# Attention of a mixer put in another order, and matmul results held in PSUM tiles of two banks

## The chip, the cores and the metric

One core of one Trainium2 chip runs the whole program. The metric is the device time of one execution in microseconds (us), the median of several runs. A separate execution of the same program was profiled; all rows below come from that one.

## The reference

A trunk of two layers over 256 tokens of width 1024, all float32. Each layer is: half a SwiGLU block (width 2816), a hybrid mixer, half a SwiGLU block; a last RMSNorm ends it. Cut to the mixer:

```python
def hybrid_mixer(h, w_in, b_forget, g_kv, w_kv_up, g_idx_k, w_up_fox, w_up_sb, w_up_dsa, w_out, cos, sin):
    (q_a, k_a, v_a, f_a, q_b, k_b, v_b, q_c, c_kv, q_i, k_i, w_i, gates) = jnp.split(h @ w_in, _split_points(), axis=-1)
    y_a = forgetting_attention(heads(q_a, N_HEADS_FOX), heads(k_a, N_HEADS_FOX), heads(v_a, N_HEADS_FOX), f_a + b_forget)
    y_b = stick_breaking_attention(heads(q_b, N_HEADS_SB), heads(k_b, N_HEADS_SB), heads(v_b, N_HEADS_SB))
    k_c, v_c = jnp.split(rmsnorm(c_kv, g_kv) @ w_kv_up, 2, axis=-1)
    ...
    y_c = dsa_attention(q_c, k_c, v_c, q_i, k_i, w_i)
    g_a, g_b, g_c = jnp.split(jax.nn.sigmoid(gates), N_BRANCH, axis=-1)
    merged = g_a * (y_a @ w_up_fox) + g_b * (y_b @ w_up_sb) + g_c * (y_c @ w_up_dsa)
    return merged @ w_out
```

Forgetting attention ("fox" in the kernel) adds to its scores the difference of cumulated log-sigmoids of the forget logits `f_a`. Stick-breaking attention ("stick") weighs by a cumulated sum of log-sigmoids along the keys. The sparse attention ("dsa") keeps, for each query, the keys with the largest indexer scores.

## The kernel before

**Weights.** Every weight matrix is read from HBM once, in chunks of columns. SyncE's queue brings float32 pieces into four `raw` buffers; ScalarE writes their f16 high part `whi` (L251), VectorE the remainder `wlo` (L253), into seven buffers each. A piece is 128x2048 at most. TensorE multiplies activations, split the same way, by both parts: three matmuls of 256 columns for each 128x128 block of weights (`project_T`, L339), or the same with tokens as rows (`project`, L374 to L376).

**Products and PSUM.** A product of 512 weight columns fills two PSUM tiles of one bank each (`banks_of` takes two of the four buffers of `mmt`). Each tile is evicted by an instruction of its own, up to 512 columns wide: the gate (L658) and the product with the up half (L665) of the feed-forward block (FFN), the scaling of projections (L809, L811), the gating of the mixer's three up-projections (L1172). Attention scores take the two `at` buffers, the small results the two `tp` buffers.

**Order in a mixer.** The input projection `w_in` runs in eight groups (`IN_GROUPS`): indexer, dsa queries and latent, fox keys, fox queries, fox values with forget logits, stick queries, stick keys, stick values; then six chunks of gates (`gt`), the three up-projections `up` in two halves each, and the output projection `o`. Attention is written as tasks (generators); after every two k-tiles of a weight product `background()` lets each task take one step up to its next `yield`. So a task's instructions land between those of the products, and the number of `yield`s sets how far behind its inputs a step stands on each engine. The forget task (from L947) turns the forget logits into `kb` (L974) and `qb` (L977), which the first matmuls of each fox score `sa` need; the indexer task ends in eight iterations of top-k, MAX8 (L913) and MATCH_REPLACE8 (L914) on two spans each. The stick heads wait in a chain: score `sb`, three exponential and logarithm steps on ScalarE (`eb`), `lb` and `hb` (L1087, L476), cumulated sum `cb` (L1096), exp, values `yb` (L989), split into `y`. The sigmoids of the gates (L1160) come after the last of them, since they need another table of ScalarE.

**Start and end.** The first chunk's x and weights come in small pieces; of the second chunk (`ci == 1`) four pieces of 128x1024 are read. The row scale `Rf` of the first norm (L551) is copied on ScalarE during the second chunk, and the first gates (L658) need it. Gains of later norms are loaded at about 56 us (`grow`, L465) and transposed on TensorE (`gps`, L417). At the very end the last chunk of the down-projection is made with tokens as rows, first the rows of token tile 0, then those of tile 1, in two PSUM tiles `d0768` and `d1768`; each has a residual step (L695), a norm and a store.

Of the kernel before, what the change touches and what calls it, by code (L numbers as in the profile page):

```python
# [20 lines left out]
P = 128  # L21
D = 1024
SEQ = 256
# [26 lines left out]
IN_GROUPS = [(QI, 324), (QC, 448), (KA, 384), (QA, 384), (VA, 390), (QB, 384), (QB + 384, 256), (VB, 320)]  # L50
# [79 lines left out]
def trunk(ctx, tc, io, out, flag):  # L130
# [22 lines left out]
    def mmt(name):  # L153
        return pp.tile([P, 512], F32, tag="mm", bufs=4, name=name)
# [45 lines left out]
    RAW_BUFS, HL_BUFS = (4, 6) if wide else (4, 7)  # L200
# [151 lines left out]
    def banks_of(n, nm):  # L352
        return [mmt(f"{nm}_{i}") for i in range((n // P + 1) // 2)]
# [48 lines left out]
    grow0 = cp.tile([16, P], F32, tag="grow0", name="grow0")  # L402
    grow1 = cp.tile([34, P], F32, tag="grow1", name="grow1")
# [19 lines left out]
    def warm_up(n, *first):  # L423
        ps = mmt("warm")
        for i in range(n):
            behind(nc.tensor.matmul(ps[:, :P], ident, ident, start=True, stop=True), *first)
# [15 lines left out]
    def const(nm, shape, dt=F32):  # L442
# [4 lines left out]
    mask_a, mask_b, tri, negu, fsel, rope_c, rope_s = (  # L447
        late.append(const(nm, shape, dt)) or late[-1][0] for nm, shape, dt in (
            ("mask_a", [P, P], BF16), ("mask_b", [P, 2 * P], BF16), ("tri", [P, 2, SEQ], F32), ("negu", [P, P], F32),
# [6 lines left out]
             (wkv, io["w_kv_up"].rearrange("l k n -> k l n")),  # L456
             (grow1[:16, :], io["g_mix"].rearrange("l (k p) -> (l k) p", p=P)),
             (grow1[16:32, :], io["g_ffn2"].rearrange("l (k p) -> (l k) p", p=P)),
             (grow1[32:34, :], io["g_kv_latent"])]
# [22 lines left out]
    class Norm:  # L482
# [16 lines left out]
        def half(self, h):  # L499
# [3 lines left out]
            with tc.high_priority():  # L503
                for k in range(4 * h, 4 * h + 4):
                    self.parts(k, xT[:, k, :])
# [31 lines left out]
        def scales(self, ms):  # L537
# [8 lines left out]
            yield  # L546
            yield
# [88 lines left out]
    def ffn(l, gu, dn, norm, nxt):  # L636
# [4 lines left out]
        def parts(s, c, n):  # L641
            for (i, j, w), st in zip(widths(n), s):
                j += c // P
                split(ah[:, j:j + w, :], al[:, j:j + w, :], pair(st, w), 1.0 / (sw * sx), note())
                yield

        for c, n in FF_CHUNKS:
            nm = f"{gu}{l}_{c}"
            g = banks_of(n, "g" + nm)
# [12 lines left out]
            u = banks_of(n, "u" + nm)  # L662
            project_T(gu, l, DFF + c, n, (norm.hi, norm.lo), u, gate)
            for i, _, w in widths(n):
                nc.vector.tensor_tensor(s[i][:, :w * SEQ], u[i][:, :w * SEQ], s[i][:, :w * SEQ], op=ALU.mult)  # L665
            done[c // P] = Task(parts(s, c, n))
# [11 lines left out]
        if nxt is not None:  # L678
            for c, n in down_chunks(dn, l):
                d = banks_of(n, f"d{c}{dn}{l}")  # L680
                project_T(dn, l, c, n, (ah, al), d, ready)
                with tc.high_priority():
                    for i, b, w in widths(n):
                        add_T(c // P + b, w, d[i], norm.by_row(w))
                nxt.half(c // 512)
# [4 lines left out]
        for c, n in down_chunks(dn, l):  # L690
            d = [mmt(f"d{t}{c}{dn}{l}") for t in range(NT)]
# [84 lines left out]
    def mixer(l, norm, nxt):  # L776
# [12 lines left out]
        def group(c, n, parts):  # L789

            ps = [mmt(f"in{c}_{t}_{l}") for t in range(NT)]
# [10 lines left out]
        def group_T(c, n):  # L802
            ps = banks_of(n, f"in{c}_{l}")
            project_T("w_in", l, c, n, (norm.hi, norm.lo), ps)
            return ps
# [72 lines left out]
        def indexer():  # L878
# [7 lines left out]
            yield  # L886
            yield
# [3 lines left out]
            for j in range(2):  # L891
                ps = blocks(f"iqp{j}{l}", [(t, PQI + j * P, P) for t in range(NT)])
                Ts = [halves(ps, r, f"iq{j}{r}{l}") for r in (0, HD)]
                yield
# [14 lines left out]
            nc.vector.memset(sc[:CHUNK, P + 3 * CHUNK:3 * P], NEG)  # L909
            for i in range(TOPK // 8):  # L910
# [4 lines left out]
                yield  # L915
# [135 lines left out]
        def dsa_heads(heads, nm):  # L1051
# [7 lines left out]
            for _ in range(3):  # L1059
                yield  # L1060
# [8 lines left out]
        def stick_heads(heads, nm):  # L1069
# [5 lines left out]
            for _ in range(3):  # L1075
# [44 lines left out]
        for g, at, eighth in ((2, 3, False), (3, 0, True)):  # L1120
            ps = group_T(*IN_GROUPS[g])
            for i, j, w in widths(WA):
                scaled(qk[:, at + j:at + j + w, :], pair(ps[i], w), norm.by_row(w), eighth)
# [8 lines left out]
        ps = group_T(*IN_GROUPS[5])  # L1132
# [5 lines left out]
        ps = group_T(*IN_GROUPS[6])  # L1138
        scaled(qk[:, 9:11, :], pair(ps[0], 2), norm.by_row(2), False)
# [5 lines left out]
        for i in range(6):  # L1145
            ps = banks_of(512, f"gt{i}_{l}")
            project_T("w_in", l, GATES + i * 512, 512, (norm.hi, norm.lo), ps)
            for j, b, w in widths(512):
                scaled(gt[:, 4 * i + b:4 * i + b + w, :], pair(ps[j], w), norm.by_row(w), False)
# [29 lines left out]
        for h in range(2):  # L1179
            ps = banks_of(512, f"o{h}_{l}")  # L1180
            project_T("w_out", l, h * 512, 512, (mh, ml), ps)
            with tc.high_priority():
                for i in range(2):
                    xs = xT[:, 4 * h + 2 * i:4 * h + 2 * i + 2, :]
                    nc.vector.scalar_tensor_tensor(xs, pair(ps[i], 2), 1.0 / (sw * sm), xs, op0=ALU.mult, op1=ALU.add)
            nxt.half(h)
# [67 lines left out]
```

## Time and profile before

| | us |
|---|---|
| median of 3 runs (1174.01 to 1174.45) | 1174.4 |
| the profiled execution's own time | 1174.17 |
| its span in the trace | 1172.4 |
| TensorE busy | 1126.7 |
| VectorE busy | 776.4 |
| ScalarE busy | 617.2 |
[...]

Some 1.8 us of the profiled execution lie outside the span. TensorE is busy for 96% of it, but this is an average: in the FFNs it never stops, and the time in which it stands lies in the first 35 us, in the two mixers and in the last 20 us. Busy counts a matmul that runs at half the clock as well, so a stretch can be busy and slow.

### The profile page before, as it was taken

What the parts mean: (1) busy time and instruction counts of PE and PEld (TensorE: products, weight loads), DVE (VectorE), ACT (ScalarE), POOL (GpSimd) and SP (SyncE); (2) the same over time, 40 slices, a digit from 0 to 9 for tenths busy, and PEclk for the clock granted to TensorE, in tenths of its full rate; (3) what the DMA queues carried; (4) which work ended last, traced back from release to release, by engine and by line L of the source; (5) the groups of instructions that cost most, each with busy time, mean ns of one, the idle gap of its engine ahead of it and who ended that gap; (6) DMA issues with size and microseconds to landing.
All of it is one profiled execution on the core that took longest, in us unless ns stands there. A gap on an engine that the chain in (4) does not pass through costs nothing. (4 is left out here: it accounts for less than half of the span.)

```text
span 1172.4 us, 22850 instructions
## 1 busy us (share of the span) xinstructions
PE 1126.7 (96%) x9744; PEld 962.4 (82%) x9744; DVE 776.4 (66%) x1341; ACT 617.2 (53%) x833; POOL 12.9 (1%) x25
## 2 busy tenths in 40 slices
PE   9999999989998999999999999999899989999996
PEld 7888886767886888888888888867688778988765
DVE  5966556996656966575575565579856779655632
ACT  7745435756657564454444363366566575544520
POOL 0000000000000000000000000010000000000000
PEclk9999999999998999999999999999899989999999
DMA  8956656554342765576665575555533437555701
GB/s 294 371 185 200 219 167 193 168 183 159 110 144 73 246 202 169 176 236 199 213 205 167 168 250 164 162 189 184 179 118 118 144 107 253 180 163 195 245 29 40
DMA packets 118772, 209.96 MB, mean 179 GB/s; under 512 B 4819, under 2 KB 43909, under 8 KB 118661
## 3 DMA queue, kind: packets, MB, share of 16 engines
q1 hardware_dynamic: 118340, 207.88, 54.9%
q8 instruction: 78, 1.28, 0.4%
q10 hardware_dynamic: 320, 0.53, 0.1%
q14 instruction: 34, 0.27, 0.1%
HBM read 207.35 MB, written 1.05 MB: 178 GB/s over the span
## 5 line engine op out<-in xcount | busy, mean ns | idle before, releaser
L253 DVE SCALAR_TENSOR_TENSOR wlo<-raw,whi 128x2048 f16<-128x2048 f32 (+5 forms) x218 | 446.6, 2050 | 254.7 <-ACT whi L251 254.5
L339 PEld LDWEIGHTS <-whi 128*128 128x128 f16 x5504 | 539.0, 98 | 69.5 <-issue 5.9
L251 ACT ACTIVATE whi<-raw 128x2048 f16<-128x2048 f32 (+5 forms) x218 | 374.0, 1718 | 409.1 <-issue 95.7
L339 PEld LDWEIGHTS <-wlo 128*128 128x128 f16 x2768 | 271.6, 98 | 38.7 <-issue 4.8
L339 PE MATMUL gw_ffn_gu<-xThif,whi 128*128 128x256 f16 x704 | 191.6, 273 | 1.2 <-DVE s0w_ffn_gu L658 1.2
L339 PE MATMUL gw_ffn_gu<-xTlof,whi 128*128 128x256 f16 x704 | 191.7, 273 | 0.8 <-DVE xTlof L496 0.8
L339 PE MATMUL gw_ffn_gu<-xThif,wlo 128*128 128x256 f16 x704 | 191.5, 273 | 1.0 <-DVE wlo L253 0.9
L339 PE MATMUL uw_ffn_gu<-xThif,whi 128*128 128x256 f16 x704 | 191.9, 273 | 0.0
L339 PE MATMUL uw_ffn_gu<-xThif,wlo 128*128 128x256 f16 x704 | 191.9, 273 | 0.0
L339 PE MATMUL uw_ffn_gu<-xTlof,whi 128*128 128x256 f16 x704 | 191.9, 273 | 0.0
L339 PE MATMUL gt<-xTlomx,whi 128*128 128x256 f16 x384 | 104.7, 273 | 0.0
L339 PE MATMUL gt<-xThimx,wlo 128*128 128x256 f16 x384 | 104.7, 273 | 0.0
L339 PE MATMUL gt<-xThimx,whi 128*128 128x256 f16 x384 | 104.7, 273 | 0.0
L339 PE MATMUL d0w_ffn_down<-ahw_ffn_gu,whi 128*128 128x256 f16 x264 | 72.0, 273 | 0.0
L339 PE MATMUL d512w_ffn_down<-alw_ffn_gu,whi 128*128 128x256 f16 x264 | 72.0, 273 | 0.0
L339 PE MATMUL d0w_ffn_down<-ahw_ffn_gu,wlo 128*128 128x256 f16 x264 | 72.0, 273 | 0.0
L339 PE MATMUL d512w_ffn_down<-ahw_ffn_gu,whi 128*128 128x256 f16 x264 | 72.0, 273 | 0.0
L339 PE MATMUL d0w_ffn_down<-alw_ffn_gu,whi 128*128 128x256 f16 x264 | 72.0, 273 | 0.0
L339 PE MATMUL d512w_ffn_down<-ahw_ffn_gu,wlo 128*128 128x256 f16 x264 | 72.0, 273 | 0.0
L339 PE MATMUL up<-y,whi 128*128 128x256 f16 x256 | 48.6, 285 | 4.1 <-DVE gt L1172 2.5
L339 PE MATMUL in<-xThimx,whi 128*128 128x256 f16 x176 | 48.0, 273 | 0.0
L339 PE MATMUL in<-xThimx,wlo 128*128 128x256 f16 x176 | 48.0, 273 | 0.0
(329 smaller groups left out, 1393.3 us busy)
## 6 DMA issues: line engine op xcount, KB each, us to landing
raw<-in_w_ffn_gu_dram SPq DMA_DIRECT2D x60, 1024.0 KB, 5.3
raw<-in_w_ffn_down_dram SPq DMA_DIRECT2D x39, 1024.0 KB, 5.1
raw<-in_w_in_dram SPq DMA_DIRECT2D x26, 1024.0 KB, 5.1
raw<-in_w_ffn_gu_dram SPq DMA_DIRECT2D x32, 768.0 KB, 4.6
raw<-in_w_in_dram SPq DMA_DIRECT2D x12, 768.0 KB, 4.4
raw<-in_w_out_dram SPq DMA_DIRECT2D x8, 1024.0 KB, 5.1
raw<-in_w_ffn_down_dram SPq DMA_DIRECT2D x7, 512.0 KB, 3.8
raw<-in_w_in_dram SPq DMA_DIRECT2D x4, 896.0 KB, 4.8
```

Of the source, the lines that this page charges most:

```text
L251: a = nc.scalar.activation(hv, src, AF.Copy, scale=scale)
L253: return a, nc.vector.scalar_tensor_tensor(lv, src, scale, plain(hv), op0=ALU.mult, op1=ALU.subtract, **more)
L339: m = nc.tensor.matmul(o, u, v[:, k, :], start=(k == 0 and q == 0 and b % 2 == 0), stop=(end and q == len(ops) - 1))
```

## The change

The input groups are put in another order: the fox values and forget logits (`VA`) come second, and the forget task starts right after them. The indexer's top-k waits until the first fox heads have begun (`"fox" in X`), and then takes one `yield` an iteration for two. Fox, dsa and stick heads wait two steps for three before their scores; some steps elsewhere wait longer. PSUM results are held in two tiles of two banks for four tiles of one, and evicted in instructions of up to 1024 columns. The norm after a block takes its eviction as a callback (`half`). The second weight chunk is read in three pieces for four. Gains and `negu` are loaded at another place and into buffers of the shared kind.

```diff
-IN_GROUPS = [(QI, 324), (QC, 448), (KA, 384), (QA, 384), (VA, 390), (QB, 384), (QB + 384, 256), (VB, 320)]
+IN_GROUPS = [(QI, 324), (VA, 390), (QC, 448), (KA, 384), (QA, 384), (QB, 384), (QB + 384, 256), (VB, 320)]
...
     def mmt(name):
-        return pp.tile([P, 512], F32, tag="mm", bufs=4, name=name)
+        return pp.tile([P, 2, 512], F32, tag="mm", bufs=2, name=name)
...
-        cuts = [0, 1, 2, 3, 4, 6, 8] if ci == 0 else [0, 2, 4, 6, 8] if ci == 1 else list(range(0, nk, rk)) + [nk]
+        cuts = [0, 1, 2, 3, 4, 6, 8] if ci == 0 else [0, 2, 4, 8] if ci == 1 else list(range(0, nk, rk)) + [nk]
...
     def banks_of(n, nm):
-        return [mmt(f"{nm}_{i}") for i in range((n // P + 1) // 2)]
+        t = mmt(nm)
+        return [t[:, i, :] for i in range((n // P + 1) // 2)], t.rearrange("p a c -> p (a c)")[:, :n // P * SEQ]
...
     def load_late():
...
+        grow1, negu = t512("grow1")[:34, :P], t512("negu")[:, :P]
+        for r, nm, n in grow_at:
+            behind(nc.sync.dma_start(grow1[r:r + n, :], io[nm].rearrange("l (k p) -> (l k) p", p=P)), raw_dma[-1])
+        behind(nc.sync.dma_start(negu, io["negu"]), raw_dma[-1])
+        yield
...
-                for i, _, w in widths(n):
-                    st = t512(f"s{i}{nm}")
-                    nc.vector.tensor_tensor(pair(st, w), pair(g[i], w), norm.by_row(w), op=ALU.mult)
-                    last_silu["i"] = nc.scalar.activation(st[:, :w * SEQ], st[:, :w * SEQ], AF.Silu)
-                    s.append(st)
+                st = sp.tile([P, 1024], F32, tag="s1024", bufs=2, name="s" + nm)[:, :n // P * SEQ]
+                nc.vector.tensor_tensor(blocks_of(st), blocks_of(gv), norm.by_row(n // P), op=ALU.mult)
+                last_silu["i"] = nc.scalar.activation(st, st, AF.Silu)
+                s.append(st)
...
-            d = [mmt(f"d{t}{c}{dn}{l}") for t in range(NT)]
+            d = mmt(f"d{c}{dn}{l}")
+            d = [d[:, t, :] for t in range(NT)]
...
+            while "fox" not in X:
+                yield
             for i in range(TOPK // 8):
...
                     nc.vector.match_replace(out=sc[:, a:b], in_to_replace=m8, in_values=sc[:, a:b], imm_value=TAKEN)
-                yield
                 yield
...
         def fox_heads(heads, nm):
...
+            X["fox"] = True
             ops = [operands((j, h % 2 * HD), (3 + j, h % 2 * HD), f"{nm}{h}") for h in heads]
-            for _ in range(3):
+            for _ in range(2 if heads[0] else 3):
                 yield
             t_f.finish()
...
         group(*IN_GROUPS[0], [(0, 324, False, PQI)])
         t_idx = Task(indexer(), True)
-        group(*IN_GROUPS[1], [(0, WC, True, PQC), (WC, P, False, PCKV)])
+        group(*IN_GROUPS[1], [(0, WA + HA, False, PVA)])
+        t_f = Task(forget(), True)
+        group(*IN_GROUPS[2], [(0, WC, True, PQC), (WC, P, False, PCKV)])
         t_lat = Task(latent(), True)
         norm.need(True)
...
-        group(*IN_GROUPS[4], [(0, WA + HA, False, PVA)])
-        t_f = Task(forget(), True)
 
         for i, hs in enumerate(pairs(HA)):
-            Task(later(fox_heads(hs, f"a{l}"), 2 + 2 * (i == 1)))
+            Task(later(fox_heads(hs, f"a{l}"), 3 * (i == 1)))
...
-                ps = banks_of(512, f"up{b}{h}_{l}")
+                ps, pv = banks_of(512, f"up{b}{h}_{l}")
                 project_T(nm, l, h * 512, 512, yT[b], ps)
                 with tc.high_priority():
-                    for i in range(2):
-                        k = 4 * h + 2 * i
-                        v, v0 = gt[:, 8 * b + k:8 * b + k + 2, :], gt[:, k:k + 2, :]
-                        nc.vector.scalar_tensor_tensor(v, pair(ps[i], 2), 1.0 / (sw * sy), v,
-                                                       op0=ALU.mult, op1=ALU.mult)
+                    for i in range(2 if b == 2 else 1):
+                        k, w = (4 * h + 2 * i, 2) if b == 2 else (4 * h, 4)
+                        v, v0 = gt[:, 8 * b + k:8 * b + k + w, :], gt[:, k:k + w, :]
+                        u = blocks_of(pv)[:, 2 * i:2 * i + w, :]
+                        nc.vector.scalar_tensor_tensor(v, u, 1.0 / (sw * sy), v, op0=ALU.mult, op1=ALU.mult)
```

Three places show how the instructions stand. On VectorE, in the first mixer before the change, the steps from the cumulated forget logits (`cps`) to `kb` and `qb`, with a projection's scaling and a weight piece among them; the top-k iterations (`isc`) stand ahead:

```order
L914 MATCH_REPLACE isc_2401<-m_128_6_2896,isc_2401 128x256
L836 TENSOR_TENSOR Ta_2958<-pr_2222,Ta_2958 64x256
L253 SCALAR_TENSOR_TENSOR wlo_2835,sums<-raw_2705,whi_2834 128x2048
L809 SCALAR_TENSOR_TENSOR pr_2222<-in_0_0_2775,Rmx_2361 128x2x128
...
L972 SCALAR_TENSOR_TENSOR c_2902<-c_2904,c_fsel,c_2902 128x256
L837 TENSOR_TENSOR Wa_2959<-pr_2222,Ta_2958 64x256
L974 TENSOR_SCALAR kb_2913<-c_2902,c_fsel 128x256
L977 TENSOR_SCALAR qb_2915<-c_2902,c_fsel 128x256 x6
L832 TENSOR_TENSOR Ta_2966<-pr_2222,Ta_2966 64x256
```

and after it:

```order
L911 SCALAR_TENSOR_TENSOR isc_2385<-rel_0_2440,pr_2166,isc_2385 128x256
L973 CAST c_2448<-cps_2445 128x256
...
L254 SCALAR_TENSOR_TENSOR wlo_2474,sums<-raw_2305,whi_2473 128x2048
L979 SCALAR_TENSOR_TENSOR c_2448<-c_2450,c_fsel,c_2448 128x256
L825 TENSOR_TENSOR Tiq_2500<-iqp_2497,Tiq_2500 64x256
L981 TENSOR_SCALAR kb_2459<-c_2448,c_fsel 128x256
L984 TENSOR_SCALAR qb_2461<-c_2448,c_fsel 128x256 x6
L825 TENSOR_TENSOR Tiq_2503<-iqp_2497,Tiq_2503 64x256
```

The steps stood behind seven of the eight top-k iterations; now they stand ahead of all of them, between the indexer's first two scores and its last two.

On TensorE, in the first mixer before, the end of the stick heads inside the first two up-projections:

```order
L339 MATMUL up_0_1_4311<-y_2858,wlo_3694 128x256
L1096 MATMUL cb_4228<-hb_4141,negur 128x384
L151 MATMUL cb_4228<-lb_4142,negur 128x384
L151 MATMUL cb_4228<-lb_4138,negones 128x128
L1096 MATMUL cb_4234<-hb_4158,negur 128x384
L989 MATMUL yb_4242<-eb_4117,pr_2222 64x128 x3
L151 MATMUL cb_4234<-lb_4159,negur 128x384
L151 MATMUL cb_4234<-lb_4155,negones 128x128
L989 MATMUL yb_4251<-eb_4134,pr_2222 64x128 x3
L989 MATMUL yb_4251<-eb_4151,pr_2222 64x128 x3
L339 LDWEIGHTS whi_3801
L339 MATMUL up_0_0_4356<-y_2858,whi_3801 128x256
```

and after, where the last of these heads ends and the first up-projection begins:

```order
L340 MATMUL gt_0_4081<-xThimx_1823,wlo_3618 128x256
L1104 MATMUL cb_4183<-hb_4125,negur 128x384
L151 MATMUL cb_4183<-lb_4126,negur 128x384
L151 MATMUL cb_4183<-lb_4122,negones 128x128
...
L340 MATMUL gt_0_4081<-xThimx_1823,wlo_3618 128x256
L996 MATMUL yb_4213<-eb_4118,pr_2166 64x128 x3
...
L340 MATMUL up_0_4233<-y_2739,whi_3696 128x256
```

All stick heads now end inside the last gate chunk, some 24 matmuls of which stand between the last `cb` and the last `yb`, and the up-projections follow with nothing between them.

On ScalarE, at the start of the program before:

```order
L251 ACTIVATE whi_278<-raw_276 128x2048
L251 ACTIVATE whi_316<-raw_282 128x2048
L551 COPY Rf_0_420<-rbf_0_418 128x256
L251 ACTIVATE whi_358<-raw_284 128x2048
L659 ACT_TABLE_LOAD
L659 ACTIVATE s0w_ffn_gu_0_428<-s0w_ffn_gu_0_428 128x512
```

and after:

```order
L252 ACTIVATE whi_313<-raw_279 128x2048
L252 ACTIVATE whi_354<-raw_281 128x2048
L560 COPY Rf_0_448<-rbf_0_446 128x256
L252 ACTIVATE whi_384<-raw_283 128x2048
L666 ACT_TABLE_LOAD
L666 ACTIVATE sw_ffn_gu_0_445<-sw_ffn_gu_0_445 128x1024
```

The copy of `Rf` follows the second half of the second chunk's up columns (`whi_354`), where it stood behind the first half; on VectorE the gate stands one weight piece later as well, and is one instruction.

## Rows read from the trace of the kernel before

**Rows 1.** Windows: stretch, its length, busy time and count by engine, clock, DMA, GB/s.

```profile
50.00:100.00 50.00, 50.00 (x459) 44.62 (x457) 32.55 (x49) 22.35 (x23) 0.00 (x0) 1.00 0.65 214
...
175.00:250.00 75.00, 69.60 (x545) 53.98 (x543) 61.58 (x157) 44.21 (x73) 3.55 (x3) 1.00 0.59 183
...
250.00:350.00 100.00, 95.54 (x826) 80.45 (x827) 65.85 (x137) 60.37 (x132) 0.00 (x0) 0.98 0.45 143
...
350.00:400.00 50.00, 44.63 (x356) 37.03 (x355) 40.63 (x66) 33.67 (x45) 0.00 (x0) 0.93 0.36 115
```

**Rows 2.** Waits of TensorE: who waited for whom; us in total, times, longest.

```profile
PE sa L151 <- DVE qb L977: 7.8, 2, 3.9
...
PE yb L989 <- ACT eb L787: 2.9, 4, 1.2
...
PE up L339 <- DVE gt L1172: 2.5, 2, 1.3
...
PE cb L1096 <- ACT hb L476: 2.4, 2, 1.2
...
PE ikTp L844 <- DVE kin L771: 1.9, 2, 1.0
...
PE gw_ffn_gu L339 <- DVE s0w_ffn_gu L658: 1.2, 1, 1.2
```

**Rows 3.** Windows, columns as in rows 1: where the granted clock was low.

```profile
252.00:255.00 3.00, 3.00 (x16) 2.20 (x15) 2.96 (x12) 1.14 (x3) 0.00 (x0) 0.50 0.89 326
...
368.00:374.00 6.00, 4.22 (x19) 3.11 (x20) 2.53 (x6) 5.89 (x11) 0.00 (x0) 0.50 0.01 3
...
826.50:831.00 4.50, 4.50 (x22) 3.11 (x21) 4.43 (x17) 1.59 (x5) 0.00 (x0) 0.50 0.61 221
```

**Rows 4.** Timeline, first mixer: start, length, engine, line, operation, count, [idle before].

```profile
236.00 0.17 DVE L947 TENSOR_TENSOR f<-pr,bfor 128x12 f32<-128x12 f32 x1
...
251.31 1.61 DVE L977 TENSOR_SCALAR qb<-c,c_fsel 128x256 bf16<-128x256 bf16 x6
...
251.70 0.43 PE L151 MATMUL sa<-kb,qb 128*128 128x128 bf16 x2 [3.88 <-DVE qb L977]
```

**Rows 5.** Timeline, first mixer, TensorE among the first up-projections.

```profile
368.65 1.54 PE L989 MATMUL yb<-eb,pr 128*64 128x128 f32 x6 [1.20 <-ACT eb L787]
```

**Rows 6.** Groups by form: operation, count, busy us, mean ns, idle before, its causes.

```profile
L253 DVE SCALAR_TENSOR_TENSOR wlo<-raw,whi 128x2048 f16<-128x2048 f32 x133 | 304.1, 2289 | 137.6 <-ACT whi L251 137.4
...
L1172 DVE SCALAR_TENSOR_TENSOR gt<-up,gt 128x512 f32<-128x512 f32 x24 | 15.8, 684 | 9.9 <-ACT gt L1160 5.1 <-PE up L339 4.8
...
L253 DVE SCALAR_TENSOR_TENSOR wlo<-raw,whi 128x1024 f16<-128x1024 f32 x11 | 13.4, 1222 | 9.6 <-ACT whi L251 9.6
```

**Rows 7.** Timeline, start: ScalarE, VectorE and TensorE around the first gates.

```profile
29.10 0.35 ACT L551 COPY Rf<-rbf 128x256 f32<-128x256 f32 x1
...
29.97 1.91 ACT L251 ACTIVATE whi<-raw 128x2048 f16<-128x2048 f32 x1 [0.52 <-DMA raw<-in_w_ffn_gu_dram]
...
31.45 0.68 DVE L658 TENSOR_TENSOR s0w_ffn_gu<-gw_ffn_gu,Rf 128x512 f32<-128x512 f32 x1
...
32.05 0.68 DVE L658 TENSOR_TENSOR s1w_ffn_gu<-gw_ffn_gu,Rf 128x512 f32<-128x512 f32 x1
...
32.18 0.27 PE L339 MATMUL gw_ffn_gu<-xThif,whi 128*128 128x256 f16 x1 [1.23 <-DVE s0w_ffn_gu L658]
```

**Rows 8.** Window at the start, columns as in rows 1.

```profile
16.00:20.00 4.00, 4.00 (x39) 3.59 (x38) 3.72 (x9) 4.00 (x10) 0.00 (x0) 1.00 0.42 115
```

**Rows 9.** Timeline, the gains: first of three issues, transpose; DMA view: KB, us to landing.

```profile
56.03 0.50 SPq L465 DMA_DIRECT2D grow<-in_g_mix_dram  x1
...
68.63 0.25 PE L417 MATMUL gps<-ident,grow 34*128 34x34 f32 x1
...
grow<-in_g_mix_dram SPq DMA_DIRECT2D x1, 8.0 KB, 6.3
```

**Rows 10.** Timeline, end: the residual of token tile 0.

```profile
1155.01 0.48 DVE L695 SCALAR_TENSOR_TENSOR x<-d0768w_ffn_down,half,x 128x256 f32<-128x256 f32 x1 [1.83 <-PE d0768w_ffn_down L376]
```

More of the change, by code (lines that the diff above doesn't have):

```diff
@@ L199, in trunk @@
     RAW, PIECE = 2048, 1024 if wide else 2048
-    RAW_BUFS, HL_BUFS = (4, 6) if wide else (4, 7)
+    RAW_BUFS, HL_BUFS = (3, 6) if wide else (4, 7)
     raws, pieces, chunk_pieces = [], [], []
@@ L497, in parts, with half @@
                                                    op0=ALU.mult, op1=ALU.subtract))
-        def half(self, h):
+        def half(self, h, add):
             if h == 0:
@@ L504, in half @@
                 for k in range(4 * h, 4 * h + 4):
+                    if k % 2 == 0:
+                        add(k // 2 % 2)
                     self.parts(k, xT[:, k, :])
@@ L545, in scales @@
                 nc.vector.tensor_scalar(dg[:, t, :], ident, self.rstd[:, t:t + 1], None, op0=ALU.mult)
-            yield
-            yield
+            for _ in range(4):
+                yield
             ps = tpt("rb" + self.nm)
@@ L641, in parts @@
         def parts(s, c, n):
[L642 to L645, printed above, removed]
+            j, w = c // P, n // P
+            split(ah[:, j:j + w, :], al[:, j:j + w, :], blocks_of(s), 1.0 / (sw * sx), note())
+            yield
         for c, n in FF_CHUNKS:
             nm = f"{gu}{l}_{c}"
-            g = banks_of(n, "g" + nm)
+            g, gv = banks_of(n, "g" + nm)
             project_T(gu, l, c, n, (norm.hi, norm.lo), g, norm.ready)
@@ L679, in ffn @@
             for c, n in down_chunks(dn, l):
-                d = banks_of(n, f"d{c}{dn}{l}")
+                d, _ = banks_of(n, f"d{c}{dn}{l}")
                 project_T(dn, l, c, n, (ah, al), d, ready)
[L682 to L685, printed above, removed]
+                nxt.half(c // 512, lambda i: add_T(c // P + 2 * i, 2, d[i], norm.by_row(2)))
             return
@@ L789, in group @@
         def group(c, n, parts):
-            ps = [mmt(f"in{c}_{t}_{l}") for t in range(NT)]
+            ps = mmt(f"in{c}_{l}")
+            ps = [ps[:, t, :] for t in range(NT)]
             project("w_in", l, c, n, (norm.hi, norm.lo), ps)
@@ L885, in indexer @@
             rope(kin[:, :, None, :], 1, "ki" + L)
-            yield
-            yield
+            for _ in range(4):
+                yield
             M, W = key_halves(kin, "ikT")
@@ L1058, in dsa_heads @@
             ops = [(halves(ps, (h % 2) * HD, f"{nm}{h}"), *X["kc"]) for h in heads]
-            for _ in range(3):
+            for _ in range(2):
                 yield
@@ L1074, in stick_heads @@
             ops = [operands(at(HB + h), at(h), f"{nm}{h}") for h in heads]
-            for _ in range(3):
+            for _ in range(2):
                 yield
@@ L1116, in mixer @@
         t_idx = Task(indexer(), True)
-        group(*IN_GROUPS[1], [(0, WC, True, PQC), (WC, P, False, PCKV)])
+        group(*IN_GROUPS[1], [(0, WA + HA, False, PVA)])
+        t_f = Task(forget(), True)
+        group(*IN_GROUPS[2], [(0, WC, True, PQC), (WC, P, False, PCKV)])
         t_lat = Task(latent(), True)
         norm.need(True)
[L1120 to L1123, printed above, removed]
-        group(*IN_GROUPS[4], [(0, WA + HA, False, PVA)])
-        t_f = Task(forget(), True)
+        for g, at, eighth in ((3, 3, False), (4, 0, True)):
+            _, v = group_T(*IN_GROUPS[g])
+            scaled(qk[:, at:at + 3, :], v, norm.by_row(3), eighth)
         for i, hs in enumerate(pairs(HA)):
-            Task(later(fox_heads(hs, f"a{l}"), 2 + 2 * (i == 1)))
+            Task(later(fox_heads(hs, f"a{l}"), 3 * (i == 1)))
         for hs in pairs(HC):
             Task(dsa_heads(hs, f"c{l}"))
-        ps = group_T(*IN_GROUPS[5])
+        ps, _ = group_T(*IN_GROUPS[5])
         for t in range(NT):
@@ L1137, in mixer @@
         scaled(qk[HD:, 8, :], ps[1][HD:, :SEQ], norm.R[HD:, :], False)
-        ps = group_T(*IN_GROUPS[6])
-        scaled(qk[:, 9:11, :], pair(ps[0], 2), norm.by_row(2), False)
+        _, v = group_T(*IN_GROUPS[6])
+        scaled(qk[:, 9:11, :], v, norm.by_row(2), False)
         group(*IN_GROUPS[7], [(0, WB, False, PVB)])
@@ L1145, in mixer @@
         for i in range(6):
-            ps = banks_of(512, f"gt{i}_{l}")
+            ps, v = banks_of(512, f"gt{i}_{l}")
             project_T("w_in", l, GATES + i * 512, 512, (norm.hi, norm.lo), ps)
-            for j, b, w in widths(512):
-                scaled(gt[:, 4 * i + b:4 * i + b + w, :], pair(ps[j], w), norm.by_row(w), False)
+            scaled(gt[:, 4 * i:4 * i + 4, :], blocks_of(v), norm.by_row(4), False)
         for t in list(tasks):
@@ L1179, in mixer, with add @@
         for h in range(2):
-            ps = banks_of(512, f"o{h}_{l}")
+            ps, _ = banks_of(512, f"o{h}_{l}")
             project_T("w_out", l, h * 512, 512, (mh, ml), ps)
[L1182 to L1186, printed above, removed]
+            def add(i):
+                xs = xT[:, 4 * h + 2 * i:4 * h + 2 * i + 2, :]
+                nc.vector.scalar_tensor_tensor(xs, pair(ps[i], 2), 1.0 / (sw * sm), xs, op0=ALU.mult, op1=ALU.add)
+            nxt.half(h, add)
     norm = FirstNorm(0, "f1_0")
```

31 lines of the change are left out of this document (15 added, 16 removed).

## The prediction

> **What bounds the kernel now.** I read the windows first [rows 1]. In a stretch of FFN TensorE is busy 50.00 of 50 us, with VectorE at 32.55: nothing that VectorE, ScalarE or the weight traffic does there can move the end. In the first mixer (175 to 400 us) TensorE stands 5.4 us up to 250, 4.5 between 250 and 350 and 5.4 between 350 and 400, 15.3 us in all; the other mixer is the same code. So the change is worth what it does to these idle stretches, to the start and to the last 20 us.
>
> Then the waits by releaser [rows 2]: the largest is `sa` for `qb`, 7.8 us in two times, one per mixer; then four that lie close together at the end of the attention, `yb` for `eb`, `cb` for `hb`, `up` for `gt`. [...] A busy TensorE at half clock loses half of its busy time, and the idle time doesn't hold this loss. Last the timeline [rows 4]: the forget logits are there at 236.00, `qb` is begun only at 251.31, and TensorE, which has waited 3.88 us, goes on at 251.70. VectorE is not slow there, it has other things first: the order printed with the change shows top-k iterations, scalings and weight pieces ahead.
>
> **What goes.** Per mixer:
> - The `qb` wait: 3.9 us [rows 2, 4], and half of 3.0 to 4.5 busy us at half clock, 1.5 to 2.2 [rows 3]: 5.4 to 6.1, taken at 5.8. The steps from `cps` to `qb` now stand before all top-k iterations, and the forget logits are computed three input groups earlier. Of these, two alone have 72 matmuls of 256 columns each, 0.11 us a matmul (459 in 50 us [rows 1]), 15.8 us, by far more than the 3.9 missing, even where the fox heads begin some 5 us earlier. What is late next is the fox operands, below.
> - The tail: TensorE's idle of 5.4 us in 350 to 400 [rows 1], of which about 0.4 belongs to `o`, so 5.0 for the four named waits (1.2 for `yb` [rows 5], 1.2 for `up`, 1.2 for `cb` [rows 2]) and small ones; and half of the 4.22 busy us at half clock, 2.1 [rows 3]: 7.1. After the change the stick chains run under the gate chunks, where TensorE has 48 or more matmuls of 0.11 us (5.2 us) between two steps of a chain; the chain itself is exps and three VectorE steps, of the length that the waits of before show in part (two of 1.2 us with about 2 us of `up` between them). So it is covered but without much to spare; uncovered it costs what it cost before.
> Sum of what goes: 12.9 per mixer, 25.8 us.
>
> **What comes in the mixers.** The same VectorE now carries the forget chain, the indexer's scores and the first fox operands in a shorter time, and top-k after them. Five places stand nearer to their inputs than before: `ikTp` (which already waits 0.9 to 1.0 us a mixer [rows 2], now behind one more weight piece), the indexer's second `is` behind the six `qb`, the score of the fourth fox head (its `at` buffer comes free after an exp whose max is in the queue), the first `ya`, and the transposes of the next pair. The trace doesn't show these waits. Below: zero, or less by what `ikTp` loses now, since all are covered if VectorE is idle when the input arrives. Above: a step that finds a 2048-wide weight piece just begun waits all of it, 2.29 us [rows 6]. I take the middle, 1.1 each, nearest to the waits of 0.9 to 1.3 that this kernel has at such places [rows 2]: 5.5, less 1.0 that `ikTp` has already, 4.5. In `up` and `o` the eviction of a whole product is now one instruction of about 1.22 us (the row of a 1024-wide VectorE operation of the same kind [rows 6]) for two 0.60 apart [rows 7]; the first half is free 0.6 us later. Two places, 0.6 each: 1.2, with both ends at 0 and 2.29. Sum 5.7, bounds 0 and 13.7. Net per mixer 7.2 less, both: -14.4 us.
>
> **The wide evictions elsewhere.** In the FFNs a product waits for the eviction of the one before the last, and another product of 96 matmuls, 10.5 us, lies between: eviction of 1.22 us behind a weight piece of 2.29 fits three times over. Cost 0; without that cover up to 0.6 per product. At the first gate after a norm the gate waits for `R`; three such FFN starts at 0.1: +0.3. Two 512-wide evictions take 0.60 from start to start [rows 7], 1.20 together; one of 1024 takes 1.22 [rows 6]: VectorE gains nothing that I can see. [...]
>
> **Start.** Now TensorE waits 1.23 us for the first gates, at 32.18 [rows 7]. The `Rf` copy stood behind one half of the second chunk's `whi`, at 29.10; after the change it stands behind both halves, and the gate behind one more `wlo`. With the transfers as they are, the second half's `whi` starts at 29.97 and ends at 31.88, its `wlo` (2.29) would end at 34.2 or later, and the gate's 1.22 puts TensorE at 35.4 to 36.1: +3.9. Against that, the DMA engines were busy only 0.42 of the four us from 16 to 20 [rows 8], when all `raw` buffers held small pieces; with three pieces the buffers hold 1 MB more and the piece lands some 1.5 us earlier. I take +2.1, bounds 0 and 3.9.
>
> **Gains.** `gps` runs at 68.63 without a wait, 12.6 us after its first load is issued at 56.03 [rows 9]. It moves forward by 93 matmuls (10 us) to about 60.6, its loads by one transfer (2 to 3 us). It landed after 6.3 us [rows 9]: issued at 53 to 54 it is there at 59 to 60, a later one of the three some 3 us after; so from 0 to 3 us are missing: +0.5.
>
> **End.** The two token tiles of the last chunk share one PSUM tile, and in the order the first matmul of tile 1 waits for VectorE's residual of tile 0 (0.48 us, at 1155.01 [rows 10]), which before ran beside it. About 0.7 with the hand-over, all on the path; bounds 0.5 and 1.
>
> **Sum.** 1174.2 (profiled execution, 0.2 below the median) - 14.4 + 0.3 + 2.1 + 0.5 + 0.7 = 1163.4, stated as 1163.
>
> **The rivals.**
> A, the forecast: both named stretches heal, some new waits: 1163.
> B, VectorE is free in time at the five places: for it, deferring top-k takes eight iterations out of its queue just there, and VectorE is busy only 65.85 of 100 us after 250 [rows 1]; against it, the early chain is packed into about 30 us. New waits of 1.5 per mixer, start +1: 1174.2 - 2 x 11.4 + 2.5 = 1154, taken with wide bounds, 1147 to 1158.
> C, the clock falls again: waits of 1 to 2 us in five places within some 15 us look like the four of the old tail, which were followed by 6 us at 0.50 [rows 3, 5]. It costs 2 to 3.4 us per mixer, and the start's longer wait another 1.2: 1163 + 5.4 + 1.2 = 1170. For it: the cluster is as dense; against it: the single wait of `ikTp`, 0.9 to 1.0 [rows 2], was followed by none (clock 1.00 up to 250 [rows 1]).
> D, slower: the two wide tiles starve TensorE in `up`. A product there has some 33 matmuls, 3.6 us; the eviction it needs is that of the product before the last, and with a weight piece (2.29), an eviction (1.22) and an addition of the same width (1.2) in a row VectorE takes 4.7. Each of the last four products and the first two of `o` would wait 1.1, 6.6 us; the sigmoids add up to 2 for the first eviction (VectorE's `gt` step already waits 5.1 us for them [rows 6]); and the clock would be low over the rest of `up`, 10 us more. 18.6 against the 12.9 gained: 1174 + 11 + 4 = 1189. It decides once the new waits and the slow clock pass 11 us per mixer. Against it: in `up` the evictions are put ahead of weight pieces that haven't begun, and VectorE has idle time there. [...]
> E, the gain isn't one: fox begins about as much earlier as `qb` does, waits for its operands for the same time, and the tail's waits reappear at `up`'s start: 1172 to 1176.
>
> **Chances.** A 0.47, B 0.19, C 0.17, D 0.10, E 0.07. A measurement of this kernel can tell about 0.2%, 2.3 us, from no change. Faster by more: A, B and C, 0.83; within: E and the edge of C, 0.07; slower: D, 0.10. The range leaves out D, half of E and the low edge of B: 1147 to 1174.
>
> **What would show it.** Right: no `sa` wait for `qb`, clock 1.00 after it; no `yb`, `cb` waits in the last gate chunk and `up` at 0.11 us a matmul; the first gates of the second chunk at 33 to 35 us; a gap of about 0.7 us after the last tile-0 matmul. Wrong: waits above 2.3 us for fox operands or `ya`, a clock of 0.50 some 60 to 75 us into a mixer (C), low clock in `up` with waits for `gt` (D), or idle time in the FFNs, which would mean that one wide eviction holds TensorE up there.

## The result, and the profile after

The changed kernel takes 1156.3 us (median of 4 runs, 1156.0 to 1156.7) against 1174.2 of the kernel before beside it: ratio 0.9849, 95% interval 0.9832 to 0.9866. Forecast were 1163, 1147 to 1174. Its profiled span is 1154.4 us, 18.0 less.

Where the time went is read best from the starts of the stages. In the timeline, TensorE alone, these are the first matmul of the input projection and the first of the feed-forward block behind it, for both mixers, of the kernel before (start, length, engine, line, operation):

```profile
184.42 0.30 PE L374 MATMUL in<-whi,xThimx 128*128 128x324 f16 x1
409.76 0.27 PE L339 MATMUL gw_ffn_gu<-xThif,whi 128*128 128x256 f16 x1
759.02 0.30 PE L374 MATMUL in<-whi,xThimx 128*128 128x324 f16 x1
986.07 0.27 PE L339 MATMUL gw_ffn_gu<-xThif,whi 128*128 128x256 f16 x1
```

and of the changed one:

```profile
189.76 0.30 PE L379 MATMUL in<-whi,xThimx 128*128 128x324 f16 x1
403.78 0.27 PE L340 MATMUL gw_ffn_gu<-xThif,whi 128*128 128x256 f16 x1
753.03 0.30 PE L379 MATMUL in<-whi,xThimx 128*128 128x324 f16 x1
967.02 0.27 PE L340 MATMUL gw_ffn_gu<-xThif,whi 128*128 128x256 f16 x1
```

The differences of these starts give the lengths; the last column runs to the start of the last matmul (1161.90 and 1143.58).

| us | up to the first mixer | mixer 1 | between | mixer 2 | rest |
|---|---|---|---|---|---|
| before | 184.4 | 225.3 | 349.3 | 227.1 | 175.8 |
| after | 189.8 | 214.0 | 349.3 | 214.0 | 176.6 |
| difference | +5.3 | -11.3 | 0.0 | -13.1 | +0.7 |

So the mixers gave 24.4 us, the start took 5.3 back and the end 0.7 (another 0.3 lies behind the last matmul). Nothing else moved: the feed-forward blocks between the mixers agree to 0.1 us.

The waits of TensorE after (the view of rows 2):

```profile
PE gw_ffn_gu L340 <- DVE sw_ffn_gu L665: 4.1, 1, 4.1
PE sa L866 <- ACT pa L791: 4.0, 2, 2.0
PE sb L866 <- DVE eb L1107: 2.3, 2, 1.2
PE is L866 <- DVE Tiq L825: 2.1, 2, 1.1
...
PE o L340 <- ACT mT L252: 1.7, 2, 1.2
...
PE o L340 <- DVE mT L254: 1.1, 2, 0.9
PE up L340 <- DVE gt L1179: 0.9, 2, 0.5
...
PE d768w_ffn_down L379 <- DVE x L699: 0.6, 1, 0.6
```

Of [rows 2] the `qb`, `yb`, `cb` and `ikTp` rows are gone, and `up` is down from 2.5 to 0.9. The first gates wait 4.1 for 1.2. New, or grown from 0.6 us or less a mixer, are `sa` for `pa` (2.0 in each mixer), `sb` for `eb` (1.2), `is` (1.1) and `o` for the last splits of `mT`.

The windows after, on stretches like those of [rows 1] and [rows 3] (stretch, length, busy time and count by engine, clock, DMA share, GB/s):

```profile
37.00:40.00 3.00, 3.00 (x16) 2.12 (x15) 2.94 (x4) 2.71 (x3) 0.00 (x0) 0.50 0.97 360
...
190.00:265.00 75.00, 71.41 (x538) 53.98 (x535) 67.71 (x177) 50.03 (x98) 2.24 (x3) 0.98 0.57 178
265.00:315.00 50.00, 49.01 (x434) 41.65 (x434) 36.27 (x76) 35.64 (x81) 0.00 (x0) 1.00 0.45 141
315.00:365.00 50.00, 48.84 (x426) 42.03 (x424) 30.22 (x53) 32.22 (x57) 0.00 (x0) 1.00 0.38 120
365.00:404.00 39.00, 37.16 (x338) 32.64 (x336) 37.91 (x47) 22.72 (x21) 0.00 (x0) 1.00 0.68 220
```

TensorE is idle 7.6 us in the first mixer (3.6, 1.0, 1.2 and 1.8), where it was 15.3. The up-projections run at full clock. While TensorE works, three stretches of half clock are left, each of 3.4 us: one behind the first gates (37 to 40 us) and one in each mixer, behind the `sa` wait. Before, each mixer had two, 10.2 us together in the first and 13.7 in the second. The same windows laid over whole mixers part the gain: idle 15.2 and 15.5 us before and 7.6 in both after, busy 210.1 and 211.6 before and 206.4 after, with as many matmuls. So some two thirds of the gain are waits, and the rest is less work at half clock.

### The profile page after: what moved, and what is told of

The parts are those of the page before. It is cut to its first block, busy times and chain, and to the rows that moved or that the text cites. A ratio compares the mean times of both kernels' runs of the same rounds, so it can differ in the third digit from the quotient of the medians.

```text
span 1154.4 us, 22634 instructions
## 1 busy us (share of the span) xinstructions
PE 1120.1 (97%) x9744; PEld 959.5 (83%) x9744; DVE 767.0 (66%) x1215; ACT 611.9 (53%) x784; POOL 10.3 (1%) x25
## 5 line engine op out<-in xcount | busy, mean ns | idle before, releaser
L340 PE MATMUL in<-xTlomx,whi 128*128 128x256 f16 x176 | 48.0, 273 | 0.0
```

Source lines behind the costliest of these rows:

```text
L340: m = nc.tensor.matmul(o, u, v[:, k, :], start=(k == 0 and q == 0 and b % 2 == 0), stop=(end and q == len(ops) - 1))
```

## The experiments

Theory 1: the order of the steps alone makes the gain; wide evictions give nothing and cost a little at both ends. Theory 2: fewer, wider VectorE instructions clear its queue and make part of it. Further runs part the order into its pieces. All stage lengths are differences of starts as above. Six experiments have a single execution (a time without a range). Their totals are to be read with care: among the kernels whose code is the same up to the first mixer, the first gates start anywhere from 35.9 to 38.3 us. The mixers repeat far better: 214.0 in all four of the changed kernel and the one with four pieces. Where the half clock falls differently, mixers of the same code part by up to 2 us: 225.3 and 227.1 in the kernel before, with 10.2 and 13.7 us of it.

**Wide evictions alone.** The kernel before with this part (and the loads of the gains that make room for it):

```diff
-        return pp.tile([P, 512], F32, tag="mm", bufs=4, name=name)
+        return pp.tile([P, 2, 512], F32, tag="mm", bufs=2, name=name)
...
-            for i, _, w in widths(n):
-                nc.vector.tensor_tensor(s[i][:, :w * SEQ], u[i][:, :w * SEQ], s[i][:, :w * SEQ], op=ALU.mult)
-            done[c // P] = Task(parts(s, c, n))
+            nc.vector.tensor_tensor(s[0], uv, s[0], op=ALU.mult)
+            done[c // P] = Task(parts(s[0], c, n))
```

> The kernel before with the two-bank PSUM tiles and the wide evictions alone (and the loads of the gains, which make room for them); the order of the attention is the old one. Theory 1, the mixers' gain is the order's: both mixers keep their length (225 and 227 us, within 2), the last chunk is longer by 0.7, the start by about 0.6, 1174 to 1177 us. Theory 2, the gain is that of fewer and wider VectorE instructions: each mixer is shorter by 5 us or more, below 1166.

1176.3 against 1175.2, ratio 1.0009 (0.9997 to 1.0021): no change that can be told. Mixers 225.1 and 227.2, the rest 176.6 for 175.8, the part up to the first mixer 185.7 for 184.4. Theory 2 falls. Page, part 1, of this kernel:

```profile
PE 1123.6 (96%) x9744; PEld 960.1 (82%) x9744; DVE 767.8 (65%) x1217; ACT 611.6 (52%) x785; POOL 10.0 (1%) x25
```

VectorE has 124 instructions less and is busy 8.6 us less than before (767.8 for 776.4), and no stage is shorter for it.

**The order alone.** The kernel before with the moved groups, the changed steps and the deferred top-k; PSUM tiles, evictions, start pieces and loads stay:

```diff
-IN_GROUPS = [(QI, 324), (QC, 448), (KA, 384), (QA, 384), (VA, 390), (QB, 384), (QB + 384, 256), (VB, 320)]
+IN_GROUPS = [(QI, 324), (VA, 390), (QC, 448), (KA, 384), (QA, 384), (QB, 384), (QB + 384, 256), (VB, 320)]
...
+            while "fox" not in X:
+                yield
...
-            for _ in range(3):
+            for _ in range(2):
```

> The kernel before with the new order alone (input groups, forget task, deferred top-k, changed steps, the norm's four steps); one-bank tiles, 512-wide evictions and the old start pieces stay. Theory 1: mixers 11 to 13 us shorter each, no 0.7 at the end, the start near the old one since the first gates' order stays as before: 1149 to 1154 us. Theory 2: mixers shorter by less than 6 each, above 1162.

1150.2 us, ratio 0.9791 (0.9775 to 0.9807): 6 us faster than the full change. Mixers 214.4 and 212.9, the rest 176.3, up to the first mixer 185.7. The whole gain is the order's, and what the full change gives back lies mostly at the start: 189.8 for 185.7 up to the first mixer.

**The first norm's steps.** The changed kernel with

```diff
-            for _ in range(4):
+            for _ in range(2 if self.nm == "f1_0" else 4):
                 yield
             ps = tpt("rb" + self.nm)
```

> The changed kernel, but the first norm's scale waits two steps again for four. Theory 1, the start loses 5.3 us because the row scale comes two steps later: the first gates of the second chunk start at 32.5 to 33.5 us on TensorE, no half clock behind them, 1151 to 1152.5 us. Theory 2, the three larger pieces or the wide gate are the cause: they start at 34.5 or later and the time stays above 1154.

1151.7 us, ratio to before 0.9805 (0.9788 to 0.9821). In the timeline of the start of the changed kernel (start, length, engine, line, operation, [idle before and its releaser]):

```profile
27.72 1.92 ACT L252 ACTIVATE whi<-raw 128x2048 f16<-128x2048 f32 x1
...
30.33 1.91 ACT L252 ACTIVATE whi<-raw 128x2048 f16<-128x2048 f32 x1 [0.69 <-DMA raw<-in_w_ffn_gu_dram]
...
32.15 0.35 ACT L560 COPY Rf<-rbf 128x256 f32<-128x256 f32 x1
32.27 2.29 DVE L254 SCALAR_TENSOR_TENSOR wlo<-raw,whi 128x2048 f16<-128x2048 f32 x1 [0.30 <-ACT whi L252]
...
34.49 1.22 DVE L665 TENSOR_TENSOR sw_ffn_gu<-gw_ffn_gu,Rf 128x1024 f32<-128x1024 f32 x1
...
35.86 0.27 PE L340 MATMUL gw_ffn_gu<-xThif,whi 128*128 128x256 f16 x1 [4.14 <-DVE sw_ffn_gu L665]
```

and of this experiment:

```profile
30.14 0.35 ACT L560 COPY Rf<-rbf 128x256 f32<-128x256 f32 x1
31.01 1.91 ACT L252 ACTIVATE whi<-raw 128x2048 f16<-128x2048 f32 x1 [0.51 <-DMA raw<-in_w_ffn_gu_dram]
...
32.49 1.22 DVE L665 TENSOR_TENSOR sw_ffn_gu<-gw_ffn_gu,Rf 128x1024 f32<-128x1024 f32 x1
33.76 0.27 PE L340 MATMUL gw_ffn_gu<-xThif,whi 128*128 128x256 f16 x1 [2.06 <-DVE sw_ffn_gu L665]
```

With two steps the copy of `Rf` stands ahead of the last of these `whi`, and the gate ahead of its `wlo`: 2.0 us earlier for the gate, 2.1 for TensorE. Up to the first mixer 186.0 for 189.8: 1.7 more, half of the 3.4 us of half clock that the changed kernel has behind its first gates. The mean granted clock of the execution is 0.996, for 0.992. The first gates came a little later than I expected (33.8 for 33.5 at most), the time is in the range.

**The pieces at the start.** The changed kernel with the old four pieces of the second chunk:

```diff
-        cuts = [0, 1, 2, 3, 4, 6, 8] if ci == 0 else [0, 2, 4, 8] if ci == 1 else list(range(0, nk, rk)) + [nk]
+        cuts = [0, 1, 2, 3, 4, 6, 8] if ci == 0 else [0, 2, 4, 6, 8] if ci == 1 else list(range(0, nk, rk)) + [nk]
```

> The changed kernel with the second chunk read in four pieces as before. Theory 1 (the norm's steps are the cause): the first gates stay at 35 to 37 us, 1155.5 to 1158. Theory 2 (the pieces are the cause): they come at 32 to 34 us, 1151 to 1154.

First gates at 35.8, up to the first mixer 190.6, one time of 1155.1 (0.4 below the range): the pieces are not the cause. In the seven profiled kernels that have wide tiles and four steps of the first norm the first gates start at 35.8 to 38.3, in the other four and before at 32.2 to 33.8. Four steps with narrow tiles (the order alone) give 33.4, and two with wide tiles (the wide evictions alone) 33.5: each alone costs 1.2 or 1.3 for the 32.2 of before, both together 3.6 or more, also with four pieces.

ScalarE's rows show where the pieces come in. All `whi` of 2048 columns ahead of the copy of `Rf`, before (at 29.10):

```profile
23.40 1.91 ACT L251 ACTIVATE whi<-raw 128x2048 f16<-128x2048 f32 x1 [0.70 <-DMA raw<-in_w_ffn_gu_dram]
27.28 1.91 ACT L251 ACTIVATE whi<-raw 128x2048 f16<-128x2048 f32 x1 [1.97 <-DMA raw<-in_w_ffn_gu_dram]
```

and in the changed kernel (at 32.15), the rows at 27.72 and 30.33 above and these:

```profile
20.27 3.89 ACT L252 ACTIVATE whi<-raw 128x2048 f16<-128x2048 f32 x2
24.96 1.91 ACT L252 ACTIVATE whi<-raw 128x2048 f16<-128x2048 f32 x1 [0.81 <-DMA raw<-in_w_ffn_gu_dram]
```

Two before, five after, and one of the five replaces two pieces of 1024: so the copy stands two weight pieces further back, not one. With the old four pieces it is one further back (two becomes three), but that piece's `whi` starts at 30.28, and the copy comes at 32.10 all the same. With three pieces and the first norm at two steps it is one as well. With narrow tiles, or with two steps and four pieces, it is none.

**Top-k at once.** The changed kernel without the wait for the fox heads, with two steps an iteration again:

```diff
-            while "fox" not in X:
-                yield
...
+                yield
                 yield
```

> The changed kernel, but the top-k iterations start as soon as the scores are there and take two steps each, as before. Theory A, deferring top-k is what frees VectorE for the forget chain and the fox operands: qb or the fox operands are late again, each mixer 3 us longer or more (217 and above), 1162 or above. Theory B, the early forget task alone is enough, since its chain stands ahead of top-k anyway: mixers within 1.5 us of 214, 1154 to 1159.

Mixers 213.2 and 214.4, the length of the changed kernel. The one time, 1159.5, lies half a us above the range that I gave for theory B and holds a late start (first gates at 38.3). Deferring top-k is worth nothing that shows here: `sa` waits 0.7 a mixer in place of 2.0, and input projections wait 1.8 for a scaling instead.

```profile
PE in L379 <- DVE pr L816: 3.6, 2, 1.8
...
PE sa L866 <- ACT pa L791: 1.4, 2, 0.7
```

**Forget logits late.** The changed kernel with the old places of the input groups and the forget task:

```diff
-        group(*IN_GROUPS[1], [(0, WA + HA, False, PVA)])
-        t_f = Task(forget(), True)
...
+        group(*IN_GROUPS[4], [(0, WA + HA, False, PVA)])
+        t_f = Task(forget(), True)
```

> The changed kernel with the input groups and the start of the forget task in the old places; all changed steps stay. Theory A, the early group brings only the qb wait's share: TensorE waits 3 to 6 us for qb again and each mixer is 4 to 8 us longer (218 to 222), the tail stays clean, 1164 to 1172. Theory B, the tail depends on it too, since everything behind the first fox heads is pushed back: mixers at 224 to 227, 1176 or above.

Mixers 216.5 both, 2.5 longer; 1162.5. Both numbers lie below theory A's ranges, but its kind is right: the wait is back, without the tail:

```profile
PE sa L151 <- DVE qb L984: 5.8, 2, 2.9
```

It costs less than I put for theory A (4 to 8), since the `sa` wait for `pa`, whose exp frees the buffer of the fourth head's score, falls from 2.0 to 0.4 a mixer at the same time: behind a late `qb` that buffer is free almost in time.

**The heads' steps.** The changed kernel, all heads waiting three steps, fox beginning at the old ones:

```diff
-            Task(later(fox_heads(hs, f"a{l}"), 3 * (i == 1)))
+            Task(later(fox_heads(hs, f"a{l}"), 2 + 2 * (i == 1)))
...
-            for _ in range(2):
+            for _ in range(3):
```

> The changed kernel, but fox, dsa and stick heads wait three steps each again before their scores and the fox heads begin at the old steps. Theory A, these steps bring the tail's share: waits in the up-projections come back, each mixer 5 to 8 us longer (219 to 222), 1166 to 1172. Theory B, group order and top-k bring it all: mixers within 2 us of 214, 1153 to 1160.

Mixers 227.2 and 227.3, 1185.4 us: 13 a mixer, more than either theory said. The mixers are as long as those with everything in the old order (225.1 and 227.2 with the wide evictions alone), although the forget logits come early; that the total is above the kernel before comes mostly from the start (192.2 up to the first mixer, for 184.4). So the early forget logits bring 2.5 a mixer with the heads' new steps and, as far as these kernels can be compared, nothing without them (the other one has the old steps of the indexer and of top-k too). Its waits:

```profile
PE sa L866 <- ACT pa L791: 7.6, 2, 3.8
...
PE up L340 <- DVE y L254: 5.6, 4, 1.9
PE yb L996 <- ACT eb L791: 2.9, 4, 1.2
PE cb L1104 <- ACT hb L483: 2.2, 2, 1.1
```

and a window in its first up-projections:

```profile
379.00:383.50 4.50, 4.40 (x21) 3.15 (x21) 3.66 (x4) 4.50 (x10) 0.00 (x0) 0.50 0.02 4
```

The `yb`, `cb` and half-clock rows of [rows 2, 3] are back (2.9, 2.2 for 2.4, and 0.50), and the fox wait of 3.8 us is there under another name.

**Norms at two steps, old tiles.** The order alone, with two steps for four in the norms of the feed-forward blocks:

```diff
-            for _ in range(4):
+            for _ in range(4 if self.nm.startswith("mx") else 2):
                 yield
             ps = tpt("rb" + self.nm)
```

> The kernel before with the new order alone (the second experiment), and the norms of the feed-forward blocks wait two steps again for four; those of the mixers keep four. If the norm's steps are what is left at the start (33.4 us for 32.2) and at two other blocks' starts (0.4 each), the first gates come at 32.2 to 32.5 us and the time is 1147.5 to 1149.5, below every kernel so far. If these come from the new place of other work, it stays at 1150 to 1151.

1149.8 us (1148.6 to 1151.7), ratio 0.9788 (0.9774 to 0.9801); with the order alone it was 0.9791. First gates at 33.2 for 33.4, the blocks' starts unchanged (349.7 between the mixers for 349.6). The time lies between the two ranges, so the starts decide: the steps of these norms are not what is left there. Why a start after a mixer takes 0.3 longer than before stays open. Both versions beat the kernel before and the changed one, and can't be told apart.

**Dsa and stick steps alone.** Only the six tasks of the dsa and stick heads wait three steps again:

```diff
         def dsa_heads(heads, nm):
...
-            for _ in range(2):
+            for _ in range(3):
```

> The changed kernel, but the dsa and stick heads wait three steps each again before their scores; the fox heads keep the new steps. Theory A, these waits push the stick chains into the up-projections: waits of yb, cb and up come back there with half clock, each mixer 6 to 10 us longer (220 to 224), 1168 to 1176, while the fox scores wait no longer than 2.3 us. Theory B, the fox heads' beginning sets where the whole row of heads ends: mixers within 2.5 us of 214.

Mixers 214.8 both, 0.8 longer; 1158.8. Theory A falls, though `up` waits for `y` a little:

```profile
PE up L340 <- DVE y L254: 2.2, 2, 1.1
```

**Fox steps alone.** Only the fox heads get their old steps:

```diff
-            Task(later(fox_heads(hs, f"a{l}"), 3 * (i == 1)))
+            Task(later(fox_heads(hs, f"a{l}"), 2 + 2 * (i == 1)))
...
-            for _ in range(2 if heads[0] else 3):
+            for _ in range(3):
```

> The changed kernel, but the fox heads begin at the old steps and wait three; dsa and stick heads keep the new ones. Theory A: the 3.8 us wait of the fox scores comes back with its half clock, 3 to 6 us a mixer (217 to 220), and the tail stays clean. Theory B, the heads stand in one row, so a later start of fox pushes the stick chains into the up-projections all the same: mixers 221 or above.

Mixers 219.3 and 218.3, 4.8 longer on the mean; 1167.3, as theory A has it. `sa` for `pa` is at 3.8 a mixer, with a half clock behind it (window as above):

```profile
PE sa L866 <- ACT pa L791: 7.6, 2, 3.8
```

```profile
263.00:266.00 3.00, 3.00 (x14) 1.78 (x12) 3.00 (x7) 1.33 (x5) 0.00 (x0) 0.50 0.57 216
```

Neither half of the steps gives 13 us: 0.8 and 4.8 make 5.6. What joins them is the place where the row of heads ends. Measured from the first `in` matmul of the first mixer:

| kernel | last `yb` at | first `up` at | mixer 1, us |
|---|---|---|---|
| changed | 168.5 | 168.7 | 214.0 |
| dsa and stick steps old | 174.5 | 166.6 | 214.8 |
| fox steps old | 178.9 | 171.0 | 219.3 |
| all steps old | 184.8 | 165.4 | 227.2 |
| before | 185.4 | 165.2 | 225.3 |

The delays of the last `yb` add (6.0 and 10.4 alone, 16.3 together), the costs don't. Up to some 8 us inside the up-projections the last heads cost little. At 19 to 20 us `yb`, `cb` and the up-projections that need them wait in the open (rows above): some 7.6 us more than what the two parts cost alone. In the first mixer about half of this is idle time of TensorE (15.9 us, for 9.7 and 10.2 in the two parts and 7.6 in the changed kernel). The other half is slow work: from 377.2 to 384.0 us, among the up-projections, the granted clock is 0.50 (matmuls of `up` 0.21 us apart, 0.11 after it), and the mean granted clock of the whole execution is 0.982, for 0.994 and 0.989 in the two parts. The heads' tasks stand in one row, two at a time, so a step saved at the front is a step earlier for all behind it. That the end of the row is what joins the parts is read from this table; no run moved that end by itself. The steps of the indexer and of the mixers' norms, which the change altered too, were not tried alone.

## Why the prediction was right, and where its terms were off

The direction, the range and the kind of gain held: time left the mixers and came back at the start and the end. By its steps:

- **What goes (12.9 a mixer).** The `qb` wait and the cluster of waits in the tail are gone, as forecast. The reason given for `qb` holds (late forget logits bring the wait back), that for the tail too, with the steps of all heads as its cause. How the 12.9 was split between the two was wrong: with the forget logits late a mixer loses 2.5, not the 5.8 put down for `qb`, and the heads' steps, to which I gave no share of their own, carry 13. The two share waits: a head that is late behind `qb` is late without it, until the steps change.
- **What comes in the mixers (5.7 a mixer, net -7.2).** Oversized. The mixers fell by 11.3 and 13.1, so the new waits are less than half of it. Idle time in the first mixer went from 15.3 to 7.6. `ikTp`, which I let wait on, waits no more (probably since the indexer now lets four steps pass before it, for two); the first `ya` and the next transposes cost 0.3 at most in the changed kernel. `sa` of the fourth fox head (2.0 a mixer), `is` (1.1, of which it had 0.6 before) and `o` (1.4) came as named; `sb` for `eb` (1.2 for 0.5) was not named.
- **Deferring top-k.** Rival B counted it as a reason why VectorE would be free. Undone, it changes no mixer by more than 0.8.
- **Wide evictions.** Cost 0 in the feed-forward blocks holds to 0.1 us, also at their starts, where I had put +0.3. A 1024-wide eviction takes 1.22, the value taken from the `wlo` row. VectorE does gain, where I saw nothing in two rows: with the wide evictions alone it is busy 8.6 us less (767.8 for 776.4) with 124 instructions less, 0.07 each by the profile's busy times, and no stage became shorter by it. Taken singly, two of 0.68 and one of 1.22 us differ by 0.14; queued, the two start 0.60 apart, and most of this is gone.
- **Start (+2.1).** The kind of mechanism, the row scale's copy behind more `whi`, the gate behind more `wlo`, was right; the term was mis-sized: +5.3, outside its bounds of 0 and 3.9. I counted one more piece ahead of the copy, and read the printed orders so; the rows have two. The piece that I counted did land earlier, by more than the 1.5 us reckoned: its `whi` starts at 27.72, where it started at 29.97. But the copy stands behind the next one too, which starts at 30.33, and the first gates came 3.7 later. The rest, 1.6, is half clock behind the 4.1 us wait (37 to 40 us), which I had only in a rival. What makes the copy late I had not seen either: the norm's four steps for two, together with the wide tiles.
- **Gains (+0.5).** No wait of `gps` shows: 0.
- **End (+0.7).** Right: 0.7. The rows at the end of the changed kernel, the residual and the first matmul of token tile 1, [idle before]:

```profile
1135.95 0.48 DVE L699 SCALAR_TENSOR_TENSOR x<-d768w_ffn_down,half,x 128x256 f32<-128x256 f32 x1 [1.83 <-PE d768w_ffn_down L381]
...
1136.49 0.27 PE L379 MATMUL d768w_ffn_down<-whi,ahw_ffn_gu 128*128 128x256 f16 x1 [0.58 <-DVE x L699]
```

- **The rivals.** B (VectorE in time at the five places, 11.4 less a mixer, 1154) was nearest, in the mixers and in the sum, though not by its reason, the deferred top-k. E did not come in the changed kernel, but it is what the heads' old steps give: the wait of 3.8 under another name, and the tail again. D did not come: in `up` TensorE waits 0.5 a mixer at full clock, with the two wide tiles, and no run shows the 10 us of low clock that D counted for them: the clock of the changed kernel is 1.00 from 365 to 404 us. C came in part: a half clock of 3.4 us behind the `sa` wait of each mixer, which cost next to nothing (last section), and one at the start.

So the total was 7 us too high by two errors of opposite sign: the new waits in the mixers about 10 us too large over both, the start 3 too small. That it came this near to the time is in part luck.

## What to carry to other kernels

When tasks are woven into the products by counting steps, look where the whole row ends against the work that can hide it: parts that cost 1 and 5 us alone cost 13 together once nothing was left to hide behind. Undo a change in its parts before keeping it whole: here the order alone is 6 us faster than order and wide evictions together. Where two wide tiles take the place of four narrow ones, look at both ends of the program, where one instruction now holds what two released one after the other.

## What the runs showed of the hardware

The same wait of 2.0 us in the fox scores was followed by half clock in the changed kernel and by none in the one with two steps for the first norm:

```profile
255.26 0.55 PE L866 MATMUL sa<-Wa,Ta 128*128 128x256 f32 x1 [1.99 <-ACT pa L791]
```

```profile
255.00:259.00 4.00, 3.74 (x18) 2.71 (x19) 4.00 (x15) 3.52 (x7) 0.00 (x0) 0.57 0.22 32
```

```profile
251.49 0.39 PE L866 MATMUL sa<-Wa,Ta 128*128 128x256 f32 x1 [1.98 <-ACT pa L791]
...
260.68 1.25 PE L996 MATMUL ya<-pTa,pr 128*64 128x128 f32 x12 [0.98 <-ACT pTa L1025]
...
266.17 0.33 PE L1023 MATMUL ppa<-ident,pa 128*128 128x128 f32 x1 [0.82 <-ACT pa L791]
```

```profile
251.00:255.00 4.00, 3.51 (x29) 2.95 (x30) 4.00 (x13) 3.76 (x7) 0.00 (x0) 1.00 0.17 29
```

The first two blocks are the changed kernel: the wait, then a granted clock of 0.57 over the four us around and behind it (0.50 for 3.4 of them); TensorE runs 18 matmuls there. The last two are the other kernel, whose times are 3.8 us earlier: the same wait, a clock of 1.00, 29 matmuls in as long a stretch, and in place of the slow work two waits for ScalarE, 0.98 and 0.82. Both mixers take the same time, 214.0 and 213.9. VectorE is busy in all of both windows, so there the slow clock seems to have cost nothing: TensorE would have stood for about as long. That it is VectorE and ScalarE that set the pace in this stretch is argued from these rows, and was not tried by a run of its own.

Elsewhere the half clock did cost time. In the kernel before the two mixers are the same code, with TensorE idle for 15.2 and 15.5 us; with 10.2 us at half clock the first takes 225.3, with 13.7 the second 227.1. In the order alone they take 214.4 and 212.9 us; the clock is at half for 6.8 us of the first (253.8 to 260.6; 0.53 from 255 to 261) and for 3.4 us of the second.
